# Half of the feed-forward products by Strassen's method, braided with plain ones

## The chip, the core and the metric

The kernel runs on one core of one Trainium2 chip. The metric is device microseconds of one execution. Three runs of the kernel before took 2767.71, 2767.93 and 2768.26 us; the median is 2767.93 us.

## The reference

Two transformer blocks run one after the other on 256 tokens of width 2048, all in float32. Only the feed-forward parts bear on the change:

```
h2 = rmsnorm(x, ffn_norm_g)                                  # first block, D_FF = 5632
x  = x + (silu(h2 @ w_ffn_gate) * (h2 @ w_ffn_up)) @ w_ffn_down

h  = rms_norm(x, g_ff)                                       # second block, D_FF_2 = 8192
x  = x + square(relu(h @ w_ff1)) @ w_ff2
```

`w_ffn_gate`, `w_ffn_up` and `w_ff1` have 2048 rows, so these are the products with K=2048. Ahead of them stand attention, pooling and gates, which the change leaves as they are.

## The kernel before, in words

Every float32 product is made of three fp32r products (`mm3`, L197 to L199): an operand is split into a high part, which fp32r holds exactly, and a low part, which is the rest. x_high w_high + x_high w_low + x_low w_high are added up in PSUM.

The weights come in **pieces** of 256 rows and 512 columns (512 KB). A piece is loaded to a `raw` buffer by a DMA on SP's queue; ScalarE casts it to the high part `wh` (L167); VectorE subtracts to get the low part `wl` (L172); TensorE then does 12 matmuls of 512 columns with it (two K tiles, two token tiles, three products each), with the activations as the stationary operand. A **chunk** is 512 columns of a weight: eight pieces for K=2048, and then an eviction of its two PSUM banks.

All orders are written out by hand (`tc.manual_schedule`). The list `jobs` holds pieces and closures; `drive` walks it, and before the matmuls of piece k it issues the splits up to piece k+4 (`LA`). So on ScalarE's and VectorE's queues the splits of the next four pieces always stand ahead of the eviction that follows piece k. There are five buffers for each of `wh` and `wl`, four PSUM banks for chunks (`acc`) and four for transposes and attention (`aux`).

In the first block's feed-forward, chunks of gate and up alternate, in groups of 4, 4 and 3 pairs; after a pair, its 256 x 512 result is transposed by TensorE (L243, eight transposes to two `aux` banks) and split again, and after a group comes the part of `w_ffn_down` that belongs to it (four chunks of 16 or 12 K tiles). In the second block, four groups of four chunks of `w_ff1` are each followed by four chunks of `w_ff2`. Up's eviction is a VectorE instruction (L750); in the second block ScalarE does the Relu (L1047) and VectorE the square (L1048).

Of the kernel before, what the change touches and what calls it, by code (L numbers as in the profile page):

```python
# [15 lines left out]
P = 128  # L16
S = 256
# [7 lines left out]
LA = 4  # L25
# [43 lines left out]
def body(tc, d, out):  # L69
# [4 lines left out]
    with tc.manual_schedule(), \  # L74
         tc.tile_pool(name="res", bufs=1) as res, \
         tc.tile_pool(name="raw", bufs=RAW) as rawp, \
         tc.tile_pool(name="wh", bufs=LA + 1) as whp, \
         tc.tile_pool(name="wl", bufs=LA + 1) as wlp, \
         tc.tile_pool(name="acc", bufs=4, space=bass.MemoryType.PSUM) as accp, \
         tc.tile_pool(name="aux", bufs=4, space=bass.MemoryType.PSUM) as auxp:  # L80
# [10 lines left out]
        posi = res.tile([P, NT], I32, name="posi")  # L91

# [29 lines left out]
        nacc, naux = [0], [0]  # L122

        def acc_tile():
            nacc[0] += 1
            return accp.tile([P, 512], F32, tag="acc", name=f"acc{nacc[0]}")

        def aux_tile():
            naux[0] += 1
            return auxp.tile([P, 512], F32, tag="aux", name=f"aux{naux[0]}")  # L130

# [6 lines left out]

        def drive():
            pcs = [j for j in jobs if j[0] == "pc"]  # L140
            raws, hl = {}, {}
            nd, ns = [0], [0]

            def dma(upto):
                while nd[0] <= min(upto, len(pcs) - 1):
# [5 lines left out]
                    t = rawp.tile([P, 1024], F32, tag="raw", name=f"raw{i}")  # L151
                    v = t[:, : a * n].rearrange("p (a b) -> p a b", a=a)
                    sync.dma_start(v, src)
                    raws[i] = v
                    nd[0] += 1

            def split(upto):
                while ns[0] <= min(upto, len(pcs) - 1):
                    i = ns[0]
                    dma(i + RAW - 1)  # L160
                    if i in before_split:
                        before_split[i]()
                    v = raws.pop(i)
                    a, n = v.shape[1], v.shape[2]
                    h = whp.tile([P, 1024], F32R, tag="wh", name=f"wh{i}")
                    hv = h[:, : a * n].rearrange("p (a b) -> p a b", a=a)
                    act.copy(hv, v)  # L167
                    lv = None
                    if pcs[i][3]:
                        l = wlp.tile([P, 1024], F32R, tag="wl", name=f"wl{i}")  # L170
                        lv = l[:, : a * n].rearrange("p (a b) -> p a b", a=a)
                        dve.tensor_tensor(lv, v, hv.bitcast(F32), op=ALU.subtract)  # L172
                    hl[i] = (hv, lv)
                    if pcs[i][4]:
                        pcs[i][4](hv, lv)
                    ns[0] += 1

            k = 0
            for j in jobs:
                if j[0] == "run":  # L180
                    j[1]()
                else:
                    split(k + LA)
                    j[2](*hl.pop(k))
                    k += 1

        def piece(src, fn, lo=True, post=None):
            return ("pc", src, fn, lo, post)
# [12 lines left out]
        def chunk(pair, w, kts, c0, n, evict, row0=0, inject=None):  # L201
            """items of pair.T @ w[:, c0:c0+n]; evict(tok, psum) after the last product"""
            items, banks = [], []

            def mk(j):
                def fn(h, l):
                    if j == 0:
                        banks.extend([acc_tile() for _ in range(NT)])
                    for q in range(2):
                        kt = 2 * j + q  # L210
                        for tok in range(NT):
                            mm3(banks[tok][:, :n], pair(kt, tok), (h[:, q, :], l[:, q, :]), kt == 0, kt == kts - 1)
                return fn

            for j in range(kts // 2):
                if inject and j in inject:
                    items.append(("run", inject[j]))
                items.append(piece(wsrc(w, row0 + 2 * j, c0, n), mk(j)))

            def fin():  # L220
                for tok in range(NT):
                    evict(tok, banks[tok][:, :n])
# [3 lines left out]

        def split2(dst_h, dst_l, src, scale=None):
            """dst_h + dst_l = src * scale exactly (scale: a column, or None)"""
# [7 lines left out]
        def transposed(nat, pair, kts, gain=None):  # L236
            """pair[kts] = transposes of nat(tok, i) for the i-th of kts, times gain(kt)"""
# [14 lines left out]
        def rsqrt_mean(o, ss, n):  # L252
            """o = (ss / n + EPS) ** -0.5"""
# [4 lines left out]
        def rsqrt_sum(o, ss, n):  # L258
            """o = (ss + n * EPS) ** -0.5"""
# [7 lines left out]
        # ================= start =================  # L267
# [254 lines left out]
        oT = pairat(A, 0, 16)  # L522
        PS = [X[:, 0:512], X[:, 512:1024]]
# [64 lines left out]
        def s_pair(p):  # L588
# [11 lines left out]
            for h in range(2):  # L600
                for qt in range(NT):
                    j = 2 * qt + h
                    o = slice(qt * S, qt * S + P * (qt + 1))
                    dve.tensor_tensor_reduce(PS[h][:, o], banks[h][:, o], mask[:, (1 - qt) * P :], 1.0, -3e38,
                                             ALU.add, ALU.max, mx[:, j : j + 1])
            dve.scalar_tensor_tensor(nmx, mx, -1.0, rq, ALU.mult, ALU.mult)
            for h in range(2):
                for qt in range(NT):
                    j = 2 * qt + h
                    o = slice(qt * S, qt * S + P * (qt + 1))  # L610
                    act.activation(PS[h][:, o], PS[h][:, o], AF.Exp, bias=nmx[:, j : j + 1], scale=rq[:, j : j + 1],
                                   accum_out=sm[:, j : j + 1])
            dve.reciprocal(rs, sm)
            for h in range(2):
                for qt in range(NT):
                    j = 2 * qt + h
                    o = slice(qt * S, qt * S + P * (qt + 1))
                    dve.tensor_scalar(PS[h][:, o], PS[h][:, o], rs[:, j : j + 1], None, ALU.mult)

        def pt_pair(p):  # L620
            for h in range(2):
                bank = aux_tile()
                for c, o in ((1, 3 * P), (2, 0), (3, 2 * P)):
                    pe.transpose(bank[:, c * P : (c + 1) * P], PS[h][:, o : o + P], ident)  # L624
# [11 lines left out]

        tmp = res.tile([P, 512], F32, name="tmp")
# [55 lines left out]
        def wide(pair, w, ev, tr, pending, kts=16, inject=None, row0=0):  # L693
            """four chunks of 512 columns; the transposes of a chunk run inside the next one"""
# [35 lines left out]
        def t_x(pair, gname):  # L730
            def mk(c):
                return lambda: transposed(lambda tok, i: xnat[:, tok, c * 512 + i * P : c * 512 + (i + 1) * P],
# [4 lines left out]
        pending = wide(mixT, "w_out", ev_res(G[:, 7680:8192], inv2), t_x(h2T, "ffn"), pending)  # L737

# [1 line left out]
        abuf = [rview(G, 1024 * i, NT, 512) for i in range(2)]  # L740

        def ev_silu(c):
            def f(tok, ps):
                act.activation(abuf[c % 2][:, tok, :], ps, AF.Silu, scale=inv2[:, tok : tok + 1])
            return f

        def ev_up(c):
            def f(tok, ps):
                a = abuf[c % 2][:, tok, :]
                dve.scalar_tensor_tensor(a, ps, inv2[:, tok : tok + 1], a, ALU.mult, ALU.mult)  # L750
            return f

        def t_a(aT, c, j):
            return lambda: transposed(blocks(abuf[c % 2]), aT, list(range(4 * j, 4 * j + 4)))
# [10 lines left out]
        for gi, (c0, nch) in enumerate(groups):  # L765
            aT = pairat((C, B)[gi % 2], 0, 16)
            for j in range(nch):
                c = c0 + j
                inj = {}
                if pending is not None:  # L770
                    inj[3 if gi == 0 and j == 0 else 2] = pending
# [375 lines left out]
```

## Time and profile before

| | |
|---|---|
| span of the profiled execution (its own time is not listed apart from it) | 2766.2 us |
| median of the three timed runs | 2767.93 us |
| TensorE busy, of the span | 2759.2 us (100%) |
| weight loads / VectorE / ScalarE busy | 81% / 54% / 47% |
| mean granted TensorE clock | 0.999 |
| DMA | 506.47 MB, 183 GB/s |

TensorE's matmuls overlap one another (each lasts 0.39 us and the next starts 0.23 us after it), so its busy share says only that it hardly ever stands still. Idle time of another engine costs nothing here as long as TensorE waits for none.

### The profile page before, as it was taken

The page shows a single profiled execution, that of the slowest core. Times are in us where ns is not written, and L with a number is a line of the kernel's source. Part 1 is how long each engine was busy: PE and PEld are TensorE (multiplying, and loading weights), DVE is VectorE, ACT ScalarE, POOL GpSimd, SP SyncE. Part 2 cuts the span into 40 slices and gives each one's busy share as a digit, 9 for nine tenths or more (in the row PEclk, how much of TensorE's full clock was granted, in tenths as well). Part 3 has the DMA queues.
Part 4 walks back from the last instruction along what each step waited for, and adds up shares of the span by engine and source line. Part 5 has one row for each costly group of instructions (what it writes and reads, how often), then busy time and mean ns, then how long its engine had stood idle before and what let it go on. Part 6 is the DMA issues. An engine that isn't in the chain of part 4 may idle for free.

```text
span 2766.2 us, 32868 instructions
## 1 busy us (share of the span) xinstructions
PE 2759.2 (100%) x12628; PEld 2249.2 (81%) x12628; DVE 1502.3 (54%) x1717; ACT 1289.0 (47%) x1682; POOL 71.8 (3%) x153
## 2 busy tenths in 40 slices
PE   9999999999999999999999999999999999999999
PEld 8988888888888888888888888888888888888887
DVE  6554677755445454445555475455555455455553
ACT  6544666544443344334455555544444344343442
POOL 1000111000000000000000010000000000000000
PEclk9999999999999999999999999999999999999999
DMA  7665444555555555555555555555555555555554
GB/s 257 214 208 196 158 138 143 176 181 177 190 184 189 185 181 189 184 189 183 183 184 168 191 183 170 181 184 187 181 179 182 190 183 183 188 179 188 183 184 151
DMA packets 143165, 506.47 MB, mean 183 GB/s; under 512 B 16160, under 2 KB 18592, under 8 KB 142496
## 3 DMA queue, kind: packets, MB, share of 16 engines
q1 hardware_dynamic: 142864, 504.31, 53.5%
q8 instruction: 99, 1.62, 0.2%
q14 instruction: 58, 0.48, 0.1%
q10 hardware_dynamic: 144, 0.05, 0.0%
HBM read 502.21 MB, written 2.10 MB: 182 GB/s over the span
## 4 chain that ended last, share of the span: by engine, by line
PE 100%; DMA 0%; DVE 0%; ACT 0%; SPq 0%; issue 0%
PE acc L197 32%; PE acc L198 32%; PE acc L199 31%; PE aux L243 2%; PE aux L197 1%; PE aux L198 1%; PE aux L199 1%; PE aux L578 0%; PE aux L624 0%; DMA raw<-in_w_in_dram 0%; PE aux L461 0%; PE aux L585 0%; PE aux L871 0%; PE aux L867 0%; PE aux L482 0%; PE aux L483 0%
## 5 line engine op out<-in xcount | busy, mean ns | idle before, releaser
L172 DVE TENSOR_TENSOR wl<-raw,wh 128x1024 fp32r<-128x1024 f32 (+2 forms) x947 | 1141.3, 1212 | 1023.4 <-ACT wh L167 1017.6
L167 ACT CAST wh<-raw 128x1024 fp32r<-128x1024 f32 (+1 forms) x950 | 978.4, 1037 | 1091.6 <-PE acc L199 1062.5
L197 PE MATMUL acc<-wh,A 128*128 128x512 f32 (+2 forms) x2336 | 920.6, 394 | 0.7 <-ACT wh L167 0.7
L198 PE MATMUL acc<-wl,A 128*128 128x512 f32 (+2 forms) x2336 | 917.1, 393 | 0.8 <-DVE wl L172 0.8
L199 PE MATMUL acc<-wh,A 128*128 128x512 f32 (+2 forms) x2336 | 917.0, 393 | 0.0
L199 PEld LDWEIGHTS acc<-wh,A 128*128 128x128 f32 x2336 | 438.2, 188 | 102.7
L197 PEld LDWEIGHTS acc<-wh,A 128*128 128x128 f32 x2336 | 438.5, 188 | 100.5 <-ACT wh L167 0.8
L198 PEld LDWEIGHTS acc<-wl,A 128*128 128x128 f32 x2336 | 438.6, 188 | 100.4 <-DVE wl L172 1.1
L197 PE MATMUL acc<-wh,B 128*128 128x512 f32 (+1 forms) x768 | 301.5, 393 | 0.0
L199 PE MATMUL acc<-wh,B 128*128 128x512 f32 (+1 forms) x768 | 299.7, 390 | 0.0
L198 PE MATMUL acc<-wl,B 128*128 128x512 f32 (+1 forms) x768 | 299.7, 390 | 0.0
L197 PE MATMUL acc<-wh,C 128*128 128x512 f32 x672 | 266.6, 397 | 0.0
L199 PE MATMUL acc<-wh,C 128*128 128x512 f32 x672 | 265.5, 395 | 0.0
L198 PE MATMUL acc<-wl,C 128*128 128x512 f32 x672 | 265.4, 395 | 0.0
L197 PEld LDWEIGHTS acc<-wh,B 128*128 128x128 f32 x768 | 144.0, 187 | 32.6
L199 PEld LDWEIGHTS acc<-wh,B 128*128 128x128 f32 x768 | 143.9, 187 | 32.3
L198 PEld LDWEIGHTS acc<-wl,B 128*128 128x128 f32 x768 | 144.1, 188 | 31.6
L199 PEld LDWEIGHTS acc<-wh,C 128*128 128x128 f32 x672 | 125.9, 187 | 30.9
L197 PEld LDWEIGHTS acc<-wh,C 128*128 128x128 f32 x672 | 126.0, 187 | 30.2
L198 PEld LDWEIGHTS acc<-wl,C 128*128 128x128 f32 x672 | 126.0, 188 | 30.1
L230 ACT CAST B<-aux 128x512 fp32r<-128x512 f32 (+1 forms) x56 | 30.1, 575 | 47.3 <-PE aux L243 43.9
L231 DVE TENSOR_TENSOR B<-aux,B 128x512 fp32r<-128x512 f32 (+1 forms) x56 | 35.6, 666 | 29.2 <-ACT B L230 29.2
(191 smaller groups left out, 1149.7 us busy)
## 6 DMA issues: line engine op xcount, KB each, us to landing
raw<-in_w_ff_dram SPq DMA_DIRECT2D x256, 512.0 KB, 3.2
raw<-in_w_in_dram SPq DMA_DIRECT2D x224, 512.0 KB, 4.1
raw<-in_w_ffn_gate_dram SPq DMA_DIRECT2D x88, 512.0 KB, 3.2
raw<-in_w_ffn_up_dram SPq DMA_DIRECT2D x88, 512.0 KB, 3.2
raw<-in_w_ffn_down_dram SPq DMA_DIRECT2D x88, 512.0 KB, 3.2
raw<-in_w_out_dram SPq DMA_DIRECT2D x64, 512.0 KB, 3.3
raw<-in_w_attn_o_dram SPq DMA_DIRECT2D x32, 512.0 KB, 4.0
raw<-in_w_kv_b_dram SPq DMA_DIRECT2D x16, 512.0 KB, 3.4
```

Of the source, the lines that this page charges most:

```text
L167: act.copy(hv, v)
L172: dve.tensor_tensor(lv, v, hv.bitcast(F32), op=ALU.subtract)
L197: pe.matmul(o, x[0], w[0], start=first, stop=False)
L198: pe.matmul(o, x[0], w[1], start=False, stop=False)
L199: pe.matmul(o, x[1], w[0], start=False, stop=last)
L230: act.copy(dst_h, src)
L231: dve.tensor_tensor(dst_l, src, dst_h.bitcast(F32), op=ALU.subtract)
L243: pe.transpose(bank[:, (2 * j + tok) * P : (2 * j + tok + 1) * P], nat(tok, b + j), ident)
```

## The change

**The method.** For `w_ffn_up` and for every second chunk of `w_ff1`, a piece is treated as a 2 x 2 matter: two K tiles by two token tiles of the activations, two K tiles by two halves of 256 columns of the weights. Eight block products become seven (Strassen's method in the form with the fewest additions). Each is three matmuls of 256 columns: a Strassen piece has 21 matmuls of 256 columns, a plain one 12 of 512.

**What the method needs.** VectorE makes four sums of the weight's blocks in place in the loaded piece (three instructions, L203 to L205), so the split is 1792 columns wide for 1024. The activations' four sums are made once (`transposed_s`, into `forms`). The seven products gather in PSUM banks 0 to 3, and after the eighth piece one ScalarE copy and four VectorE additions (L323 to L327) put them together; then comes the eviction.

**The order.** A plain chunk (pieces M0 to M7) and a Strassen chunk (S0 to S7) are braided: M0 M1 S0 M2 S1 M3 S2 M4 S3 M5 S4 M6 S5 M7, eviction of the plain chunk, S6 S7, eviction of the Strassen chunk. There are 11 such braids in the first block and 8 in the second (two to a group). The transposes of the braid before run ahead of S1; in the second block they are those of both chunks, four banks full.

**The buffers.** `wh` and `wl` become one array `W` with slots at fixed places: three slots for M pieces, two for S pieces, and six for pieces outside of braids, which lie on the same ground. The splits run up to three pieces ahead in a braid and four outside, but only as far as the slot's last user is done. In a braid banks 0 to 3 are the Strassen chunk's, 4 and 5 the plain one's, and 6 and 7 are left for transposes. The first chunk after a braid uses banks 2 and 3. Relu and square of the second block are now both ScalarE instructions (L1182, L1183).

```diff
+AHEAD = {PLAIN: 4, MIX: 3, STR: 3}
...
+        FREE = {PLAIN: [0, 1, 2, 3], MIX: [4, 5]}
+        AUX = {PLAIN: (4, 5, 6, 7), MIX: (6, 7)}
...
+        def hslots(kind, n):
+
+            if kind == STR:
+                return (n % 2) * 1792, (2 + n % 2) * 1792, 1792
+            s = n % (3 if kind == MIX else 6)
+            o = 7168 + 1024 * s if s < 3 else 1024 * (s - 3)
+            return o, o + 3072, 1024
...
+            def sums(upto):
+
+                while nt[0] <= min(upto, nd[0] - 1):
+                    i = nt[0]
+                    if pcs[i][5] == STR:
+                        v = raws[i].rearrange("p (a b) -> p a b", a=8)
+                        dve.tensor_tensor(v[:, 4:6, :], v[:, 0:4:3, :], v[:, 1::-1, :], op=ALU.subtract)
+                        dve.tensor_tensor(v[:, 6, :], v[:, 3, :], v[:, 4, :], op=ALU.subtract)
+                        dve.tensor_tensor(v[:, 7, :], v[:, 2, :], v[:, 6, :], op=ALU.subtract)
+                    nt[0] += 1
+
             def split(upto):
-                while ns[0] <= min(upto, len(pcs) - 1):
+                while ns[0] <= min(upto, len(pcs) - 1) and free_h[ns[0]] <= used[0]:
...
+                    sums(i + 2)
...
+        def strassen(pair, forms, w, kts, c0, evict):
...
+            prod = [(("x", 0, 0), 0, 2, 1), (("x", 1, 0), 1, 0, 0), (("s", 3), 2, 3, 0), (("x", 1, 1), 6, 2, 0),
+                    (("s", 0), 3, 1, 1), (("s", 1), 5, 0, 1), (("s", 2), 4, 1, 0)]
...
+                        pe.matmul(o, xh, h[:, wi, :], start=first, stop=False, skip_group_check=True)
+                        pe.matmul(o, xl, h[:, wi, :], start=False, stop=False, skip_group_check=True)
+                        pe.matmul(o, xh, l[:, wi, :], start=False, stop=last, skip_group_check=True)
...
+                act.copy(v[:, 0, :], q[:, 5, :])
+                dve.tensor_tensor(u[:, 0:2, :], v[:, 0:1, :].to_broadcast(bc), q[:, 0:2, :], op=ALU.add)
+                dve.tensor_tensor(u[:, 2:4, :], u[:, 1:2, :].to_broadcast(bc), q[:, 2:4, :], op=ALU.add)
+                dve.tensor_tensor(v[:, ::-1, :], u[:, 2:3, :].to_broadcast(bc), q[:, 3:5, :], op=ALU.add)
+                dve.tensor_tensor(u[:, 3, :], u[:, 3, :], q[:, 6, :], op=ALU.add)
+                evict(0, u[:, 0:4:3, :])
+                evict(1, v)
...
+        def braid(a, b, inject=None):
+
+            pa, pb = [x for x in a if x[0] == "pc"], [x for x in b if x[0] == "pc"]
+            order = [pa[0], pa[1]]
+            for i in range(6):
+                order += [pb[i], pa[i + 2]]
+            order += [a[-1], pb[6], pb[7], b[-1]]
+            for at in sorted(inject or {}, reverse=True):
+                order.insert(at, ("run", inject[at]))
+            return order
...
+                jobs.extend(braid(chunk(h2T, "w_ffn_gate", KT, c * 512, 512, ev_silu, kind=MIX),
+                                  strassen(h2T, h2F, "w_ffn_up", KT, c * 512, ev_up),
+                                  {4: pending} if pending is not None else None))
...
+        def relu2(o, tok, v):
+            act.activation(o, v, AF.Relu, scale=inv4[:, tok : tok + 1])
+            act.activation(o, o, AF.Square)
...
+                jobs.extend(braid(chunk(h2T, "w_ff1_2", KT, c * 512, 512,
+                                        lambda tok, ps: relu2(abuf[:, tok, :], tok, ps), kind=MIX),
+                                  strassen(h2T, h2F, "w_ff1_2", KT, (c + 1) * 512, lambda tok, v: relu2(v, tok, v)),
+                                  {4: pending} if pending is not None else None))
+                pending = two(t_a(aT, blocks(abuf), j), t_a(aT, half, j + 1))
```

**VectorE, second block, where one chunk of `w_ff1` gives way to the next.** In the kernel before, the square (L1048) is followed by two low parts, then by the low parts of the two transposed banks (L231).

```order
L172 TENSOR_TENSOR wl_15490<-raw_15432,wh_15488 128x1024
L1048 TENSOR_TENSOR G<-G 128x512 x2
L172 TENSOR_TENSOR wl_15512<-raw_15450,wh_15510 128x1024
L172 TENSOR_TENSOR wl_15532<-raw_15468,wh_15530 128x1024
L231 TENSOR_TENSOR C<-aux_15546,C 128x512
L231 TENSOR_TENSOR C<-aux_15553,C 128x512
```

In the changed kernel, from the last addition that puts the Strassen chunk together (L327), the rows are the low part of M2, the sums for S2, the low part of S1, that of M3, the sums for S3, the low part of S2, and the four transposed banks (L370).

```order
L327 TENSOR_TENSOR G<-G,PS 128x256
L228 TENSOR_TENSOR W<-R,W 128x1024
L203 TENSOR_TENSOR G<-G 128x512
L204 TENSOR_TENSOR G<-G 128x256
L205 TENSOR_TENSOR G<-G 128x256
L228 TENSOR_TENSOR W<-G,W 128x1792
L228 TENSOR_TENSOR W<-R,W 128x1024
L203 TENSOR_TENSOR G<-G 128x512
L204 TENSOR_TENSOR G<-G 128x256
L205 TENSOR_TENSOR G<-G 128x256
L228 TENSOR_TENSOR W<-G,W 128x1792
L370 TENSOR_TENSOR B<-PS,B 128x512 x4
```

The banks' low parts now stand behind three splits and two sets of sums, and there are four of them on two banks.

**ScalarE at the same place.** Before, the Relu of a chunk stands between casts that were issued ahead.

```order
L167 CAST wh_15652<-raw_15596 128x1024
L1047 ACTIVATE G<-acc_15514,st 128x512
L1047 ACTIVATE G<-acc_15515,st 128x512
L167 CAST wh_15674<-raw_15614 128x1024
L167 CAST wh_15694<-raw_15632 128x1024
L230 CAST C<-aux_15710 128x512
L230 CAST C<-aux_15717 128x512
```

In the changed kernel, the cast of S0 of the next braid is followed by the copy of one product (L323), Relu and square of both token tiles (L1182, L1183), and only then by the cast of M2.

```order
L226 CAST W<-G 128x1792
L323 COPY tmp<-PS 128x256
L1182 ACTIVATE G<-G,st 128x2x256
L1183 ACTIVATE G<-G 128x2x256
L1182 ACTIVATE tmp<-tmp,st 128x512
L1183 ACTIVATE tmp<-tmp 128x512
L226 CAST W<-R 128x1024
L226 CAST W<-G 128x1792
```

Four ScalarE instructions that read what VectorE's additions give now stand ahead of M2's cast.

**VectorE at the end of the first group of the first block**, where `w_ffn_down` begins. Before, the low parts of four of its pieces stand ahead of the eviction of the last chunk (L750).

```order
L172 TENSOR_TENSOR wl_6853<-raw_6795,wh_6851 128x1024
L172 TENSOR_TENSOR wl_6871<-raw_6813,wh_6869 128x1024
L172 TENSOR_TENSOR wl_6889<-raw_6831,wh_6887 128x1024
L172 TENSOR_TENSOR wl_6907<-raw_6849,wh_6905 128x1024
L750 SCALAR_TENSOR_TENSOR G<-acc_6781,st,G 128x512
L750 SCALAR_TENSOR_TENSOR G<-acc_6782,st,G 128x512
```

In the changed kernel, the low parts of S6 and S7 are followed by the additions and by the eviction (L888), and all pieces of `w_ffn_down` stand behind them.

```order
L228 TENSOR_TENSOR W<-G,W 128x1792 x2
L324 TENSOR_TENSOR G<-tmp,PS 128x512
L325 TENSOR_TENSOR G<-G,PS 128x512
L326 TENSOR_TENSOR tmp<-G,PS 128x2x256
L327 TENSOR_TENSOR G<-G,PS 128x256
L888 SCALAR_TENSOR_TENSOR G<-G,st 128x512
L888 SCALAR_TENSOR_TENSOR G<-tmp,st,G 128x512
L228 TENSOR_TENSOR W<-R,W 128x1024 x8
```

No piece of the next weight is split ahead here, since its slot lies on ground that S7 still uses.

## Rows read from the trace of the kernel before

**Rows 1.** The page: engines' busy time and share, and the chain's engines.

```profile
PE 2759.2 (100%) x12628; PEld 2249.2 (81%) x12628; DVE 1502.3 (54%) x1717; ACT 1289.0 (47%) x1682; POOL 71.8 (3%) x153
PE 100%; DMA 0%; DVE 0%; ACT 0%; SPq 0%; issue 0%
```

**Rows 2.** Busy time by stretch: one pair of gate and up with its transposes.

```profile
core 0: us, PE busy (x) PEld busy (x) DVE busy (x) ACT busy (x) POOL busy (x), PEclk, DMA share, GB/s
714.25:759.92 45.67, 45.67 (x202) 36.82 (x201) 22.21 (x20) 19.01 (x20) 0.00 (x0) 1.00 0.52 184
```

**Rows 3.** Timeline of a feed-forward stretch: start, duration, instruction, idle before it.

```profile
1199.63 0.39 PE L199 MATMUL acc<-wh,B 128*128 128x512 f32 x1
...
1200.06 1.05 ACT L167 CAST wh<-raw 128x1024 fp32r<-128x1024 f32 x1 [1.75 <-PE acc L199]
...
1201.14 1.23 DVE L172 TENSOR_TENSOR wl<-raw,wh 128x1024 fp32r<-128x1024 f32 x1 [1.57 <-ACT wh L167]
...
1202.86 1.05 ACT L167 CAST wh<-raw 128x1024 fp32r<-128x1024 f32 x1 [1.75 <-PE acc L199]
```

**Rows 4.** The chain: start, length, link.

```profile
125.97 1.87 PE aux L461 x16
...
536.47 0.87 PE aux L243 x8
```

**Rows 5.** Timeline of the weight loads at L461.

```profile
125.58 2.06 PEld L461 LDWEIGHTS aux<-wh,C 128*128 128x128 f32 x16
```

**Rows 6.** VectorE's groups by shape: count, total us, mean ns, idle before.

```profile
L172 DVE TENSOR_TENSOR wl<-raw,wh 128x1024 fp32r<-128x1024 f32 x907 | 1105.0, 1225 | 1001.6 <-ACT wh L167 995.9
...
L172 DVE TENSOR_TENSOR wl<-raw,wh 128x768 fp32r<-128x768 f32 x24 | 22.7, 965 | 12.4 <-ACT wh L167 12.4
...
L1048 DVE TENSOR_TENSOR G<-G 128x512 f32<-128x512 f32 x32 | 22.1, 692 | 8.4 <-ACT G L1047 8.3
...
L750 DVE SCALAR_TENSOR_TENSOR G<-acc,st,G 128x512 f32<-128x512 f32 x22 | 15.4, 743 | 0.0
L723 DVE TENSOR_TENSOR X<-X,acc 128x512 f32<-128x512 f32 x24 | 15.3, 680 | 0.0
...
L417 DVE TENSOR_TENSOR X<-X 128x256 f32<-128x256 f32 x8 | 3.4, 425 | 0.3
```

**Rows 7.** ScalarE's groups by shape.

```profile
L167 ACT CAST wh<-raw 128x1024 fp32r<-128x1024 f32 x909 | 946.7, 1048 | 1072.5 <-PE acc L199 1050.3 <-issue 8.8 <-DMA raw<-in_w_in_dram 8.1
...
L167 ACT CAST wh<-raw 128x768 fp32r<-128x768 f32 x24 | 19.4, 831 | 7.4 <-PE acc L199 7.4
...
L441 ACT ACTIVATE G<-G 128x512 f32<-128x512 f32 x16 | 10.1, 632 | 14.6 <-DVE G L440 14.3
...
L230 ACT CAST C<-aux 128x256 fp32r<-128x256 f32 x8 | 3.0, 373 | 19.8 <-PE aux L199 19.8
```

**Rows 8.** VectorE's timeline where it has work queued: each row's second number spans all of its xcount.

```profile
44.96 0.20 DVE L338 TENSOR_SCALAR G<-G 128x64 f32<-128x64 f32 x1
45.19 0.20 DVE L339 TENSOR_SCALAR G<-G 128x64 f32<-128x64 f32 x1
...
61.29 3.57 DVE L172 TENSOR_TENSOR wl<-raw,wh 128x768 fp32r<-128x768 f32 x4 [0.24 <-ACT wh L167]
```

**Rows 9.** DMA issues: KB of one, median us from issue to landing.

```profile
raw<-in_w_ff_dram SPq DMA_DIRECT2D x256, 512.0 KB, 3.2
```

**Rows 10.** Timeline of the kernel's start: a wait of TensorE.

```profile
7.76 0.69 PE L198 MATMUL acc<-wl,A 128*128 128x512 f32 x1 [0.76 <-DVE wl L172]
```

**Rows 11.** Busy time by stretch at the start, columns as in Rows 2 (PEclk: granted clock).

```profile
7.00:8.00 1.00, 0.24 (x2) 0.24 (x2) 1.00 (x2) 0.26 (x1) 0.00 (x0) 0.95 1.09 413
8.00:9.00 1.00, 1.00 (x3) 0.81 (x3) 0.50 (x2) 0.06 (x1) 0.00 (x0) 0.50 1.00 376
9.00:10.00 1.00, 1.00 (x4) 0.71 (x4) 0.00 (x0) 1.00 (x2) 0.00 (x0) 0.50 1.10 402
10.00:12.00 2.00, 2.00 (x8) 1.57 (x7) 1.98 (x3) 1.84 (x4) 0.00 (x0) 0.67 1.05 387
12.00:14.00 2.00, 2.00 (x10) 1.63 (x9) 2.00 (x4) 1.82 (x4) 0.00 (x0) 1.00 1.05 385
```

More of the change, by code (lines that the diff above doesn't have):

```diff
@@ L75, in body @@
          tc.tile_pool(name="res", bufs=1) as res, \
[L76 to L80, printed above, removed]
+         tc.tile_pool(name="psum", bufs=1, space=bass.MemoryType.PSUM) as psp:
         A = res.tile([P, 8192], F32R, name="A")
@@ L207, in fn @@
                     if j == 0:
-                        banks.extend([acc_tile() for _ in range(NT)])
+                        banks.extend([FREE[kind].pop(0) for _ in range(NT)])
                     for q in range(2):
@@ L217, in chunk, with mk, fn, fin @@
                     items.append(("run", inject[j]))
-                items.append(piece(wsrc(w, row0 + 2 * j, c0, n), mk(j)))
+                items.append(piece(wsrc(w, row0 + 2 * j, c0, n), mk(j), kind=kind))
             def fin():
                 for tok in range(NT):
-                    evict(tok, banks[tok][:, :n])
+                    evict(tok, bank_at(banks[tok])[:, :n])
+                FREE[kind].extend(banks)
             items.append(("run", fin))
             return items
+        def strassen(pair, forms, w, kts, c0, evict):
+            items = []
+            prod = [(("x", 0, 0), 0, 2, 1), (("x", 1, 0), 1, 0, 0), (("s", 3), 2, 3, 0), (("x", 1, 1), 6, 2, 0),
+                    (("s", 0), 3, 1, 1), (("s", 1), 5, 0, 1), (("s", 2), 4, 1, 0)]
+            def mk(j):
+                def fn(h, l):
+                    opened = set()
+                    for x, wi, bank, half in prod:
+                        o = PS[:, bank * 512 + half * QW : bank * 512 + (half + 1) * QW]
+                        if x[0] == "x":
+                            xh, xl = pair(2 * j + x[1], x[2])
+                        else:
+                            xh, xl = forms[:, 0, j, x[1], :], forms[:, 1, j, x[1], :]
+                        first = j == 0 and bank not in opened
+                        opened.add(bank)
+                        last = j == kts // 2 - 1
+                        pe.matmul(o, xh, h[:, wi, :], start=first, stop=False, skip_group_check=True)
+                        pe.matmul(o, xl, h[:, wi, :], start=False, stop=False, skip_group_check=True)
+                        pe.matmul(o, xh, l[:, wi, :], start=False, stop=last, skip_group_check=True)
+                return fn
+            for j in range(kts // 2):
+                items.append(piece(wsrc(w, 2 * j, c0, 512), mk(j), kind=STR))
+            def fin():
+                q = PS[:, 0:2048].rearrange("p (a b) -> p a b", a=8)
+                u = rview(G, 1024, 4, QW)
+                v = tmp.rearrange("p (a b) -> p a b", a=2)
+                bc = [P, 2, QW]
+                act.copy(v[:, 0, :], q[:, 5, :])
[5 more added lines that the diff above has]
+                evict(1, v)
+            items.append(("run", fin))
+            return items
@@ L736, in body, with ev_silu, ev_up, t_a @@
         h2T = pairat(A, 0, KT)
[L737 to L754, printed above, removed]
+        h2F = rview(C, 0, 2, KT // 2, 4, P)
+        pending = wide(mixT, "w_out", ev_res(tmp, inv2), t_x(h2T, "ffn", h2F), pending)
+        abuf = rview(G, 0, NT, 512)
+        def ev_silu(tok, ps):
+            act.activation(abuf[:, tok, :], ps, AF.Silu, scale=inv2[:, tok : tok + 1])
+        def ev_up(tok, v):
+            a = abuf[:, tok, :].rearrange("p (a b) -> p a b", a=2)
+            dve.scalar_tensor_tensor(a, v, inv2[:, tok : tok + 1], a, ALU.mult, ALU.mult)
+        def t_a(aT, nat, j):
+            return lambda: transposed(nat, aT, list(range(4 * j, 4 * j + 4)))
         def ev_acc(c):
```

173 lines of the change are left out of this document (116 added, 57 removed).

## The prediction

> **What bounds the kernel now.** I read the page first: TensorE is busy for the whole span and the chain of waits is all TensorE [rows 1]. Then the stretches: a pair of gate and up takes 45.67 us, in which VectorE works 22.2 and ScalarE 19.0 [rows 2]. The timeline says how the three fit together: one plain piece every 2.80 us (from cast to cast, 1200.06 to 1202.86), a cast that waits for TensorE to give a slot back and starts 0.04 us after the releasing matmul ends (1199.63 + 0.39), then the low part 1.08 us behind it [rows 3]. So TensorE sets the pace, and the splits run four pieces ahead with half their time to spare. The change takes work from TensorE and gives it to the two others; the question is whether they still come in time.
>
> **What it saves.** A plain piece is 12 matmuls in 2.80 us, 0.233 us each. For 256 columns the chain has 16 matmuls in 1.87 us, 0.117 us each, with a new weight load for each [rows 4]. So a Strassen piece takes 21 x 0.117 = 2.46 us, 0.34 less. There are 19 braids of eight such pieces: 152 x 0.343 = **52.1 us saved**. Eight transposes take 0.87 us as before [rows 4].
>
> One reading speaks against this. A load lasts 0.19 us, and the 16 loads of those 256-column matmuls take 2.06 us together, not 3.0: they overlap one another [rows 5]. The Trainium skill (Perfetto Trace Analysis, Identifying the Most-Contended Engine) says that matmul busy time is a bad measure of headroom and that the busy share of LDWEIGHTS should be used. Taken that way, a Strassen piece would cost its loads; I price that as a rival below. The row is nearer to this change than the rule, so I go by the row.
>
> **Prices on the other engines.** VectorE: 1024 columns 1.225 us, 768 columns 0.965, so 1792 come to 1.225 + 3 x 0.26 = 2.0; the three sums are 0.692 + 2 x 0.425 = 1.54; an addition from PSUM 0.68; up's eviction 0.743 [rows 6]. ScalarE: 1024 columns 1.048 and 768 columns 0.831, so 1792 come to 1.70; an activation from SBUF 0.632; 256 columns from PSUM 0.373 [rows 7]. Four low parts of 768 columns in a row take 3.57 us, not 3.86, so an instruction that needs nothing of the one before starts 0.10 us early; one that needs it starts 0.03 us late (44.96 + 0.20 to 45.19) [rows 8]. The trace has no 1792-column instruction; the two shapes bound the slope, so I add nothing to the range for it. In a queue a plain low part is then 1.13 us, a Strassen one 1.91, its sums 1.50: a pair needs 4.53 of VectorE against 5.26 of TensorE. With additions, up's eviction and transposes, VectorE has about 41 us of work in a braid of 42.9. That is enough in total; what decides is the order in the queues. A weight's DMA lands 3.2 us after issue [rows 9], and a raw slot is given back more than 4.5 us (two low parts and a set of sums) before it is needed, so I cost the DMAs, and the activations' sums ahead of the plain chunks, at nothing.
>
> **Where TensorE waits.** Let T be when TensorE is through with S7. The slot of S7 is that of S5, done 7.72 us before T (M7, S6, S7 follow). From there VectorE needs 0.2 for the release, 1.70 for the cast, 1.91 for S7, 1.50 for sums, 2.25 for M0 and M1, 1.50 for sums and 2.0 for S0: 11.1 us, so the additions begin only at T + 3.4, and end at T + 5.8 (2.43 us, three of them dependent).
>
> *First block, braids after the first (8).* The eviction (1.42) and M2's low part (1.13) bring it to T + 8.4; TensorE needs that after M0, M1, S0 and one matmul, at T + 8.3. Wait 0.2: **1.6 us** in all. The later pieces have more room.
>
> *Second block, second braid of a group (4).* Relu and square start when the additions end: four times 0.66, then M2's cast 1.05 and low part 1.23: T + 10.8, a wait of 2.5. Then TensorE does M2 and fills the two banks left for transposes (T + 14.2). The third bank must wait until VectorE has read the first, and that read stands behind sums, S1, M3, sums and S2: 1.50 + 1.91 + 1.13 + 1.50 + 1.91 = 7.9 from T + 10.8, and 0.69 for the read: T + 19.4. A wait of 5.2. S1 starts at T + 20.5 rather than T + 12.6. **7.9 each, 31.6 us.**
>
> *Ends of groups (7).* With no piece of the next weight split ahead, it stands behind copy, additions, eviction and its own split: first block 0.6 + 2.4 + 1.4 + 1.2 = 5.6, second block 0.6 + 2.4 + 2.7 (Relu, square) + 1.05 + 1.2 = 8.0. TensorE needs it at 0.2, or at 3.0 where one piece is ahead; where three are, it waits only for banks 2 and 3 to be read (2.7). The order has none ahead in the first group of the first block and the second of the second; three in the second and the third; one in the other three. That is 5.4 + 2.7 + 2.6, and 5.0 + 7.8 + 2.7 + 5.0: **31.2 us.**
>
> *Starts of groups.* In the third group of the first block and the fourth of the second, M0's slot is that of the last plain piece. It then stands behind two accumulations and S0's sums (0.2 + 1.3 + 1.5 + 1.2, less the 0.2 that TensorE has): 3.9 each. In the first group of the second block the squares of the norm come ahead too, 5.4; in the first of the first block about 1.4 for the wider split of the last transposes. **14.5 us.** The other three starts have the room.
>
> *The clock.* At the start TensorE, after tiny warm-up matmuls, stands still twice, the second time for 0.76 us [rows 10]; then the granted clock is at 0.50 (1.2 of 2.4 GHz) until about 11.2 us, which costs 0.05 + 0.5 + 0.5 + 0.66 = 1.7 us [rows 11]. The change makes 11 waits of 3.9 to 7.8 us. Whether each lets the clock fall, no row shows: between nothing and 11 x 1.7 = 18.7 us. The row at the start had a weaker load before it, so I take the middle, **9 us**.
>
> **The sum.** 1.6 + 31.6 + 31.2 + 14.5 + 9 = 87.9 lost, 52.1 saved: +35.8 us. The profiled execution's own time is its span, 2766.2, so 2802.0; the median of the runs lies 1.7 above that span: **2804 us**, 1.3% slower.
>
> **The rivals.**
> *Everything hides (faster).* If the low parts that follow a braid's additions came in time, only the 52.1 would be left: 2716 us, or up to 2735 with part of the ends. For it: VectorE's and ScalarE's totals fit in a braid. Against it: the rows of order, in which these low parts stand behind the additions. It decides from the point where all waits together are under 52 us, which means additions, eviction and split some 3 us shorter than the rows make them.
> *Instructions in a queue do not overlap.* With full durations the additions begin at T + 3.8, the second block's late braids lose 8.8, the first block's 1.1: 10.5 us more, 2814; with every wait also dropping the clock, 2823. For it: many of these instructions depend on one another.
> *The third bank does not wait*, if the transposed banks are read earlier than I think: 4 x 5.2 and some of the clock less, 2779.
> *The loads bound.* 21 x 0.188 = 3.95 us for a Strassen piece, 152 x 1.15 = 175 more than a plain one instead of 52 less; the waits inside braids go, those at the ends stay: about 2980. Against it, rows 5. This is the Trainium skill's reading by LDWEIGHTS busy, named above.
> *Same.* It needs waits that add up to the saving within 5.5 us (0.2%, about what a measurement of this kernel can tell from no change); nothing ties the two together.
>
> **How the numbers follow.** The forecast as worked out (2792 to 2813): 0.55. No overlap, or a clock that falls every time (2813 to 2826): 0.19. No wait for the third bank (2774 to 2792): 0.12. Between those and no change: 0.01. Same: 0.03. Faster: 0.08. Loads bound: 0.02. The range from 2774 to 2826 holds the first three, 0.86; its low end leaves out the third-bank wait, its high end takes full durations and all 11 falls of the clock. Slower: 0.55 + 0.19 + 0.12 + 0.01 + 0.02 = 0.89; same 0.03; faster 0.08.
>
> **What would show it.** Strassen matmuls (L310 to L312) 0.117 us apart. In the second block's second braids, TensorE idle before M2 (released by VectorE's low part, with ScalarE's squares ahead of M2's cast) and before the third transposed bank, some 8 us in each. At the ends of groups, idle times of 2.6 to 7.8 us before the first matmuls of `w_ffn_down` and `w_ff2`, longest in the second group of the second block. First braids of a group near 42.1 us without waits. PEclk below 1.00 after some waits. The prediction is wrong if TensorE's idle time in the two feed-forward parts is far below 70 us, if the matmuls of 256 columns are further apart than 0.117, or if VectorE, not its order, fills the braids.

## The result and the profile after

| | before | after |
|---|---|---|
| time, median of 4 runs (us) | 2767.8 (2767.5 to 2768.3) | 2817.2 (2811.6 to 2817.9) |
| ratio, 95% interval | | 1.0175 (1.0161 to 1.0189) |
| profiled execution: time, span (us) | | 2811.6, 2809.8 |
| mean granted clock of TensorE in it | | 0.988 |

The changed kernel is 49.4 us slower; 35.8 were forecast. The profiled execution was the fastest of the four, and the only one with a mean clock of 0.988; the others show 0.985 or 0.986 and spans of 2815.4 to 2816.2. The numbers below are those of the profiled one, whose span is 43.6 us above the 2766.2 of the kernel before.

The page of the changed kernel, busy time and the chain's engines:

```profile
PE 2743.7 (98%) x13996; PEld 2300.2 (82%) x13996; DVE 1853.1 (66%) x2233; ACT 1402.6 (50%) x1749; POOL 72.9 (3%) x153
PE 5%; DVE 0%; ACT 0%; issue 0%; DVEq 0%
```

Against [rows 1] VectorE has 351 us more work and is still idle for a third of the span. The chain no longer runs through TensorE from end to end, and what the walk back covers is 5% of the span. So nothing is read from shares here. The longest waits of TensorE in the sum are these (line waited at, releaser: us in total, times, longest):

```profile
PE PS L258 <- ACT W L226: 16.9, 10, 6.0
PE PS L382 <- DVE B L370: 15.1, 4, 4.9
PE PS L258 <- DVE tmp L326: 15.1, 6, 4.1
PE PS L259 <- DVE W L228: 12.9, 13, 2.4
```

L226 is the cast of a split, L228 its low part, L326 the last but one of the additions, L370 the read of a transposed bank: the four releasers that the prediction names. A Strassen piece has the pace that was priced. Its first and last matmuls, and the plain piece behind it, in the timeline of TensorE:

```profile
722.91 0.28 PE L310 MATMUL PS<-W,A 128*128 128x256 f32 x1
723.03 0.28 PE L311 MATMUL PS<-W,A 128*128 128x256 f32 x1
723.15 0.28 PE L312 MATMUL PS<-W,A 128*128 128x256 f32 x1
...
725.25 0.28 PE L312 MATMUL PS<-W,C 128*128 128x256 f32 x1
725.37 0.39 PE L258 MATMUL PS<-W,A 128*128 128x512 f32 x1
```

From 722.91 to 725.37 are 2.46 us for 21 matmuls. Each lasts 0.28 by its modelled end and starts 0.117 behind the last: starts, not durations, give the pace.

The longest wait shows how the loss is made. The timeline at the end of the second group of the second block, from the last matmul of S7 (without the weight loads):

```profile
2312.78 0.28 PE L312 MATMUL PS<-W,C 128*128 128x256 f32 x1
2312.81 0.69 DVE L324 TENSOR_TENSOR G<-tmp,PS 128x512 f32<-128x512 f32 x1 [3.74 <-PE PS L312]
2313.61 0.69 DVE L325 TENSOR_TENSOR G<-G,PS 128x512 f32<-128x512 f32 x1
2314.33 0.69 DVE L326 TENSOR_TENSOR tmp<-G,PS 128x512 f32<-128x512 f32 x1
2314.93 0.41 DVE L327 TENSOR_TENSOR G<-G,PS 128x256 f32<-128x256 f32 x1
2315.38 0.72 ACT L1182 ACTIVATE G<-G,st 128x512 f32<-128x512 f32 x1 [2.96 <-DVE G L327]
2316.13 0.63 ACT L1183 ACTIVATE G<-G 128x512 f32<-128x512 f32 x1
2316.66 0.70 ACT L1182 ACTIVATE tmp<-tmp,st 128x512 f32<-128x512 f32 x1
2317.40 0.63 ACT L1183 ACTIVATE tmp<-tmp 128x512 f32<-128x512 f32 x1
2317.94 3.87 ACT L226 CAST W<-R 128x1024 fp32r<-128x1024 f32 x4
2319.00 2.36 DVE L228 TENSOR_TENSOR W<-R,W 128x1024 fp32r<-128x1024 f32 x2 [3.66 <-ACT W L226]
2319.02 0.79 PE L258 MATMUL PS<-W,B 128*128 128x512 f32 x1 [5.96 <-ACT W L226]
```

Read it downwards: additions, then Relu and square of two row tiles, then the first of four casts in a row, then TensorE. VectorE idled 3.74 us before the additions and 3.66 after them, ScalarE 2.96: no engine is full, one thing stands behind another. And the first matmul then lasts 0.79 where others last 0.39.

In the second braid of a second-block group TensorE waits three times. These are its rows in the first group: the last matmul of S0, the first two of M2, the first transpose on the third bank.

```profile
2078.24 0.28 PE L312 MATMUL PS<-W,C 128*128 128x256 f32 x1
2079.70 0.51 PE L258 MATMUL PS<-W,A 128*128 128x512 f32 x1 [1.18 <-ACT W L226]
2080.96 0.69 PE L259 MATMUL PS<-W,A 128*128 128x512 f32 x1 [0.75 <-DVE W L228]
...
2089.61 0.33 PE L382 MATMUL PS<-cst,G 128*128 128x128 f32 x1 [3.40 <-DVE B L370]
```

Busy time by stretch (columns as in [rows 2]), at the end of the first group of the first block and around this M2:

```profile
838.00:841.00 3.00, 0.70 (x2) 0.61 (x3) 3.00 (x4) 0.50 (x1) 0.00 (x0) 0.61 0.00 0
841.00:844.00 3.00, 3.00 (x9) 2.32 (x8) 2.65 (x3) 0.24 (x1) 0.00 (x0) 0.50 0.75 240
...
2078.00:2080.00 2.00, 0.82 (x6) 0.50 (x4) 0.32 (x1) 1.97 (x4) 0.00 (x0) 1.00 0.00 0
2080.00:2082.00 2.00, 1.25 (x4) 0.85 (x4) 1.94 (x3) 2.00 (x2) 0.00 (x0) 0.78 0.00 0
2082.00:2084.00 2.00, 2.00 (x6) 1.53 (x5) 2.00 (x2) 1.68 (x2) 0.00 (x0) 0.50 0.00 0
```

Two neighbouring matmuls of M2 three groups later:

```profile
2664.97 0.63 PE L258 MATMUL PS<-W,A 128*128 128x512 f32 x1
2665.40 0.63 PE L259 MATMUL PS<-W,A 128*128 128x512 f32 x1
```

At 2078 TensorE waits 1.2 us for M2's cast and, one matmul later, 0.8 for its low part, and then works at a clock of 0.50 (1.2 of 2.4 GHz). Three groups later the clock is at 0.50 in the same place, and matmuls of 512 columns start 0.43 us apart, where a plain piece has 0.233. The trace has 15 such stretches behind waits.

### The profile page after: what moved, and what is told of

The parts are those of the page before. It is cut to its first block, busy times and chain, and to the rows that moved or that the text cites. A ratio compares the mean times of both kernels' runs of the same rounds, so it can differ in the third digit from the quotient of the medians.

```text
span 2809.8 us, 35965 instructions
## 1 busy us (share of the span) xinstructions
PE 2743.7 (98%) x13996; PEld 2300.2 (82%) x13996; DVE 1853.1 (66%) x2233; ACT 1402.6 (50%) x1749; POOL 72.9 (3%) x153
## 3 DMA queue, kind: packets, MB, share of 16 engines
q1 hardware_dynamic: 142864, 504.31, 52.1%
## 5 line engine op out<-in xcount | busy, mean ns | idle before, releaser
L228 DVE TENSOR_TENSOR W<-R,W 128x1024 fp32r<-128x1024 f32 (+2 forms) x795 | 938.6, 1206 | 431.6 <-ACT W L226 428.8
L226 ACT CAST W<-R 128x1024 fp32r<-128x1024 f32 (+2 forms) x798 | 807.9, 1036 | 522.2 <-PE PS L260 341.1
L258 PE MATMUL PS<-W,A 128*128 128x512 f32 (+2 forms) x1728 | 682.1, 395 | 10.1 <-ACT W L226 10.1
L259 PE MATMUL PS<-W,A 128*128 128x512 f32 (+2 forms) x1728 | 682.4, 395 | 9.0 <-DVE W L228 9.0
L260 PE MATMUL PS<-W,A 128*128 128x512 f32 (+2 forms) x1728 | 680.0, 393 | 0.0
L258 PE MATMUL PS<-W,B 128*128 128x512 f32 (+1 forms) x1248 | 496.3, 398 | 21.9 <-DVE tmp L326 15.1
L259 PE MATMUL PS<-W,B 128*128 128x512 f32 (+1 forms) x1248 | 493.7, 396 | 3.9 <-DVE W L228 3.9
L260 PE MATMUL PS<-W,B 128*128 128x512 f32 (+1 forms) x1248 | 493.5, 395 | 0.0
L226 ACT CAST W<-G 128x1792 fp32r<-128x1792 f32 x152 | 257.3, 1693 | 340.5 <-PE PS L311 153.0
L259 PEld LDWEIGHTS PS<-W,A 128*128 128x128 f32 x1728 | 326.7, 189 | 81.0 <-DVE W L228 14.2
L258 PEld LDWEIGHTS PS<-W,A 128*128 128x128 f32 x1728 | 326.6, 189 | 80.0 <-ACT W L226 12.3
L260 PEld LDWEIGHTS PS<-W,A 128*128 128x128 f32 x1728 | 326.3, 189 | 74.2
L228 DVE TENSOR_TENSOR W<-G,W 128x1792 fp32r<-128x1792 f32 x152 | 307.0, 2020 | 57.4 <-ACT W L226 57.3
L258 PEld LDWEIGHTS PS<-W,B 128*128 128x128 f32 x1248 | 236.5, 190 | 78.4 <-ACT W L226 12.2
L259 PEld LDWEIGHTS PS<-W,B 128*128 128x128 f32 x1248 | 236.5, 189 | 59.4 <-DVE W L228 5.7
L260 PEld LDWEIGHTS PS<-W,B 128*128 128x128 f32 x1248 | 236.3, 189 | 55.3 <-DVE B L370 0.4
L310 PE MATMUL PS<-W,C 128*128 128x256 f32 x608 | 170.7, 281 | 0.0
L312 PE MATMUL PS<-W,C 128*128 128x256 f32 x608 | 170.6, 281 | 0.0
L311 PE MATMUL PS<-W,C 128*128 128x256 f32 x608 | 170.3, 280 | 0.0
L310 PE MATMUL PS<-W,A 128*128 128x256 f32 x456 | 130.6, 286 | 0.0
L312 PE MATMUL PS<-W,A 128*128 128x256 f32 x456 | 128.4, 281 | 0.4 <-DVE W L228 0.4
L311 PE MATMUL PS<-W,A 128*128 128x256 f32 x456 | 128.4, 282 | 0.0
```

The costliest lines, as they stand in the source:

```text
L258: pe.matmul(o, x[0], w[0], start=first, stop=False)
L259: pe.matmul(o, x[0], w[1], start=False, stop=False)
L260: pe.matmul(o, x[1], w[0], start=False, stop=last)
L310: pe.matmul(o, xh, h[:, wi, :], start=first, stop=False, skip_group_check=True)
L311: pe.matmul(o, xl, h[:, wi, :], start=False, stop=False, skip_group_check=True)
L312: pe.matmul(o, xh, l[:, wi, :], start=False, stop=last, skip_group_check=True)
```

## The experiments

Theory: the waits are made by what stands ahead in two queues at three kinds of places (second braids, ends of groups, starts of groups), each can be taken away by itself, and each costs its idle time and often a low clock behind it. Rival: VectorE has too much work in a braid, so a wait taken away comes back. A second rival concerns the clock: that it falls for another reason than the waits. Times are medians; the kernel before had 2767.4 and 2767.6 beside these runs.

| run | us | ratio to before, 95% |
|---|---|---|
| late_pending | 2790.1 | 1.0083 (1.0068 to 1.0098) |
| late_evict | 2792.9 | 1.0094 (1.0077 to 1.0111) |
| own_ground | 2764.0 | 0.9990 (0.9981 to 0.9999) |
| all_three | 2719.8 | 0.9829 (0.9814 to 0.9843) |
| plain_braid | 2767.5 | 0.9999 (0.9990 to 1.0009) |
| only_slots | 2784.6 | 1.0063 (1.0048 to 1.0078) |
| only_banks | 2804.5 | 1.0138 (1.0123 to 1.0153) |
| fill | 2795.0 | 1.0102 (1.0087 to 1.0117) |

**late_pending**: the transposes of the Strassen chunk five places later.

```diff
-                                  {4: pending} if pending is not None else None))
-                pending = two(t_a(aT, blocks(abuf), j), t_a(aT, half, j + 1))
+                                  {4: pending[0], 9: pending[1]} if pending is not None else None))
+                pending = (t_a(aT, blocks(abuf), j), t_a(aT, half, j + 1))
...
+            pending = two(*pending)
             stage(PLAIN)
```

> In the second block's second braids the eight transposes of the Strassen chunk's outputs come five pieces after the eight of the plain chunk, so that the third transposed bank no longer follows the first two at once. Order theory (each wait is made by what stands ahead in VectorE's or ScalarE's queue at that one place, and a wait costs its idle time and a fall of the clock behind it): the four idle times of 3.7 to 5.2 us before the third bank go, 16.2 us, and with them three of the falls of the clock, some 6 us: about 2795 us. Volume theory (VectorE has too much to do in a braid, so a wait taken away at one place comes back at the next): the idle time turns up again in the same braids, and the time stays within 5 us of 2817.

Measured 2790.1, 27 us less; the spans of the two executions with a trace, 2809.8 and 2788.3, are 21.5 apart. Of TensorE's waits, the line for transposed banks is gone; the others stand as they were:

```profile
PE PS L258 <- ACT W L226: 16.9, 10, 6.0
PE PS L258 <- DVE tmp L326: 14.7, 6, 3.8
PE PS L259 <- DVE W L228: 12.9, 12, 2.4
```

Waits of 15.1 us were worth 21.5 by these two traces, whose mean clocks are 0.988 and 0.990: most of the rest is the clock. Nothing came back elsewhere.

**late_evict**: the Strassen chunk's evictions one piece later.

```diff
-                evict(0, u[:, 0:4:3, :])
-                evict(1, v)
+                late.append(lambda: (evict(0, u[:, 0:4:3, :]), evict(1, v)))
...
+        def behind(items):
+            k = [i for i, x in enumerate(items) if x[0] == "pc"][0]
+            return items[: k + 1] + [("run", lambda: late and late.pop()())] + items[k + 1 :]
```

`behind` is put around each braid and each group's first plain chunk.

> The evictions of each Strassen chunk (up's product in the first block, Relu and square in the second) come after the first piece of what follows, so behind the split of that piece's successors, and no longer right behind the additions. Order theory: the waits for M2 go (4 x 2.7), the ends of the second block's groups get 2.7 us shorter each, the first end of the first block 1.4; the third bank may wait 1 us longer, since S1's cast now stands behind Relu and square; with falls of the clock about 25 us in all: 2792 us. Volume theory: within 5 us of 2817.

Measured 2792.9. The waits (L390 and L378 are the old L382 and L370):

```profile
PE PS L390 <- DVE B L378: 21.6, 4, 5.4
PE PS L258 <- DVE tmp L326: 14.7, 6, 4.1
PE PS L259 <- DVE W L228: 8.2, 7, 1.8
PE PS L258 <- ACT W L226: 7.8, 5, 2.5
```

The two lines of the split lose 13.8 us together, and the third bank waits 6.5 longer. That is not because the bank comes later, as was expected of S1's cast. In the timeline of this run the last matmul of S0 and the first on the third bank are 9.35 us apart, where they were 11.37 in the rows above:

```profile
2074.80 0.28 PE L312 MATMUL PS<-W,C 128*128 128x256 f32 x1
...
2084.15 0.47 PE L390 MATMUL PS<-cst,G 128*128 128x128 f32 x1 [5.40 <-DVE B L378]
```

The bank comes 2.0 us sooner (as much in the other three groups), but TensorE, no longer held at M2, is there sooner still. The two waits stand one behind the other, and nearly half of what the first one loses turns up in the second.

**own_ground**: slots by last use, and the gate chunk's banks for the first plain chunk.

```diff
+                if kind != STR and kind != lastk[0]:
+                    cnt[kind] = 0
+                    m = sorted(range(3), key=lambda x: seen_h.get((7168 + 1024 * x) // 256, x - 9))
+                    perm[:] = m if kind == MIX else m + [3, 4, 5]
+                    lastk[0] = kind
...
-            s = n % (3 if kind == MIX else 6)
+            s = perm[n % (3 if kind == MIX else 6)]
...
+                if m == PLAIN:
+                    FREE[PLAIN][:] = [4, 5, 0, 1]
+                    AUX[PLAIN] = (6, 7, 2, 3)
```

> At each change between braids and plain pieces the slots are taken in the order in which their last users end, and the first plain chunk after a braid takes the banks of the gate chunk (free early) instead of Strassen's. Order theory: three plain pieces are split ahead of every braid's additions, so the ends of the first block's groups lose their waits (10.4 us measured) and those of the second block keep some 2.4 us each of 20.1; the starts of groups lose about 10 of 13.4 us; with the clock about 38 us less in all: 2779 us. Volume theory: within 5 us of 2817.

Measured 2764.0, 53 us less, 15 more than expected. The waits (lines 13 further down than after the change):

```profile
PE PS L395 <- DVE B L383: 16.7, 4, 5.0
PE PS L271 <- ACT W L239: 5.3, 5, 1.2
PE PS L272 <- DVE W L241: 4.2, 6, 0.8
```

The waits for additions are gone, and those for splits fell from 29.8 to 9.5, nearly all of it M2's, which this run leaves alone. Two lines are new: 2.6 and 2.4 us, four waits each, for the split of transposed outputs, at the pieces of `w_ff2` that use them. All waits together are some 28 us less, the span 48.1. Most of the rest is the clock, whose mean is 0.995 against 0.988, and which I had put too low.

**only_slots** and **only_banks** take own_ground apart (its diff's first and second half).

> Of the change of slots and banks, the slots alone: pieces are split ahead at every change between braids and plain pieces, but the first plain chunk after a braid still takes Strassen's banks. Order theory: the starts of groups lose their waits (about 12 us) and the ends keep some 2.8 us each, the time until the additions have read the banks (19 of 30 us): 23 us of idle time less and some 10 of the clock, 2784 us. Rival (the banks make the waits at the ends, the slots matter only at the starts): 2795 or more.

> The banks alone: the first plain chunk after a braid takes the gate chunk's banks, but the slots stay as they were, so that in five of seven groups no more than one piece is split ahead. Order theory: only the ends with three pieces ahead (second group of the first block, third of the second) lose their waits, 2.8 and about 4 us, and some of the clock: 2807 us. Rival (the banks make the waits at the ends): some 20 us of idle time less, 2790 or below.

Measured 2784.6 and 2804.5, both within 3 us. With the slots alone all seven ends wait, for the additions to read the banks:

```profile
PE PS L266 <- DVE tmp L334: 18.6, 7, 3.3
```

With the banks alone that line is gone, and the splits wait longer (23.2 and 17.0 against 16.9 and 12.9):

```profile
PE PS L263 <- ACT W L231: 23.2, 12, 6.0
PE PS L264 <- DVE W L233: 17.0, 14, 4.1
```

The ends need both: together they give 53 us, alone 33 and 13.

**all_three**: the three edits above together.

> Late transposes, late evictions and slots by last use together. Order theory: nearly all of the 67 us of idle time and the 23 us that the low clock costs go, and the 53 us that the 256-column products save are left: 2720 to 2735 us, faster than the kernel before (2768). Volume theory: VectorE needs about 41 us of a braid's 42.9, so waits come back somewhere in the braids: above 2760 us.

Measured 2719.8: 97 us less than the change, and 47.6 less than the kernel before. Its page and all waits of TensorE above 0.2 us:

```profile
PE 2709.9 (100%) x13996; PEld 2279.9 (84%) x13996; DVE 1848.0 (68%) x2233; ACT 1400.3 (52%) x1749; POOL 73.9 (3%) x153
```

```profile
PE PS L271 <- ACT W L239: 1.0, 1, 1.0
PE PS L438 <- POOL nh L433: 1.0, 1, 1.0
PE PS L325 <- DVE W L241: 0.8, 2, 0.4
PE PS L272 <- DVE W L241: 0.8, 1, 0.8
```

What is left lies at the kernel's start and at the first S0 of each block. VectorE has the same work as after the change (1848 us), and nobody waits for it. The volume rival is refuted.

**plain_braid**: all_three with the second chunk of a braid by plain products.

```diff
-                                  strassen(h2T, h2F, "w_ffn_up", KT, c * 512, ev_up),
+                                  chunk(h2T, "w_ffn_up", KT, c * 512, 512,
+                                        lambda tok, ps: ev_up(tok, ps.rearrange("p (a b) -> p a b", a=2)), kind=STR),
```

The same for `w_ff1_2`; the sums and the weights' blocks are left out.

> The version with late transposes, late evictions and slots by last use, but the second chunk of each braid done by plain products (12 matmuls of 512 columns a piece, no sums, no additions, plain weights); order, slots, banks and queues of raw weights stay. It measures the saving alone. If a Strassen piece saves 21 x 0.117 against 12 x 0.233 and nothing else: 48 to 53 us above the 2719.8 of the version with all three, so 2768 to 2773, and about the kernel before. If part of the gain of that version lies in the braids or the slots themselves, it is below 2762; if Strassen's pieces saved more than their matmuls, above 2778.

Measured 2767.5, just the kernel before. So the new order, banks and slots cost and bring nothing by themselves, and Strassen's products save 47.7 us once nothing waits.

**fill**: the changed kernel with extra matmuls in the waits.

```diff
+        def busy(n, bank=6, w=None):
+            def f():
+                for _ in range(n):
+                    pe.matmul(bank_at(bank), A[:, 0:P] if w is None else w, A[:, 0:512], start=w is None, stop=w is None,
+                              skip_group_check=True)
+            return f
...
+            run(busy((9, 24, 17, 9)[gi]))
```

> The changed kernel with extra matmuls of 512 columns, whose results nobody reads (or whose weights are zero), put where TensorE waits: 10 before M2 and 14 with zero weights before the third transposed bank in the second block's second braids, 9 to 24 at the ends of groups, 6 to 11 at three starts, each set a little shorter than the wait. Clock theory (a low clock behind the waits costs some 23 us of the profiled run, and it falls because TensorE stood still): the waits stay as long, but most of those 23 us come back: 2793 to 2802 us. Rival (the clock falls for another reason, as the kind of matmul in the braids, or the low stretches are covered by work that would be waited for anyway): no gain, 2815 or more, since the extra matmuls only fill or lengthen waits.

Measured 2795.0, 22.2 us less, with 207 matmuls more. The places above by stretch, the second braid and the longest end:

```profile
2076.00:2080.00 4.00, 4.00 (x19) 3.02 (x18) 3.67 (x5) 3.69 (x4) 0.00 (x0) 1.00 0.00 0
2080.00:2084.00 4.00, 4.00 (x23) 3.37 (x22) 3.93 (x6) 1.86 (x3) 0.00 (x0) 1.00 0.52 146
2086.00:2088.00 2.00, 1.80 (x11) 1.63 (x12) 1.23 (x3) 0.86 (x2) 0.00 (x0) 0.77 0.57 162
2314.00:2318.00 4.00, 3.20 (x13) 2.08 (x12) 0.80 (x1) 3.94 (x6) 0.00 (x0) 1.00 0.00 0
```

TensorE does useless work where it stood still, the clock stays at 1.00 behind most of it, and the kernel is faster. Nothing that it waits for comes earlier: from the last matmul of S0 to the first on the third bank it is 11.4 us in all four groups of this run (2074.84 to 2086.20 in the first), as after the change; and at the longest end the first plain matmul comes 6.24 us behind the last of S7 there and 6.26 here. So the 22.2 us are the clock's alone, and the rival for the clock is refuted. The trace is of the slowest of the four executions (2800.1 us, mean clock 0.996): in it waits of up to 2.4 us are left between the first matmuls of a piece and of up to 1.7 before the third bank, and behind them five of the fifteen stretches at 0.50. The two executions at 0.999, the mean clock of the kernel before, took 2793.4 and 2793.8, so the low clock costs the changed kernel some 22 to 24 us.

## Why the prediction was right, point by point

**The saving** (52.1 forecast): 2.46 us a piece, as priced. Between plain_braid and all_three it is 47.7 us by the medians, 49.0 by the spans (2767.4, of the slowest of plain_braid's ten executions, and 2718.4). A part of the missing 3 to 4 us is at S1: in the timeline of all_three its first matmuls in a second braid start 0.20, 0.24 and 0.23 us apart behind transposes (2057.20, 2057.40, 2057.64, 2057.87) instead of 0.117. What holds them, no run took apart.

**The loads** (the rival at 2980): refuted by the same rows. The Trainium skill (Perfetto Trace Analysis, Identifying the Most-Contended Engine) would judge TensorE's room by MFU (the arithmetic done as a share of the peak) and the busy share of LDWEIGHTS. In all_three that share is 84% while TensorE waits for next to nothing, so here it did not show the bound.

**The waits** (78.9 forecast), from the list of the changed kernel's waits at each place:

| place | forecast | measured |
|---|---|---|
| first block, later braids | 1.6 | 0 |
| second block, second braids (before M2; third bank) | 31.6 (2.5 and 5.2 each) | 23.1 (8.0 and 15.1 in all) |
| ends, first block | 10.7 | 9.1 |
| ends, second block | 20.5 | 16.8 |
| starts | 14.5 | 10.0 |
| sum | 78.9 | 59.0 |

The places were right but for the first row, and so were the releasers; at M2 the cast ends the first wait and the low part the second. The list holds less than what is lost, for two reasons that are in rows. A wait is counted from a modelled end, 0.39 us after the start where the next could start after 0.233, so some 0.16 us of each is not in the list. And the low clock shortens the next wait: the third bank waits 4.9 us in the group where TensorE ran M2 at 1.00, and 3.4 in the three where it ran M2 at 0.50 and came later.

What a second braid loses is therefore better read from T, the end of S7. M0's first matmul starts at 2070.15 in the first group. M2's second matmul, which needs its low part, comes 10.8 us later and the third bank 19.5, in all four groups; T + 10.8 and T + 19.4 were forecast. Without waits the third bank would come at T + 11.7 (three plain pieces, a Strassen one, eight transposes). So these braids lose 7.7 us each, 31 in all, and this price was right, not too high. With 0.16 us for each of the other 19 waits, all waits come to 31 + 35.9 + 3, some 70 us by estimate. Too high were the ends and the starts, above all the ends of the second block with one piece split ahead (2.5 and 3.7 for 5.0); one end came out higher (4.1 for 2.7, the third group of the second block).

**The clock** (9 forecast, bounds 0 and 18.7): this is the term that was mis-sized. The balance of the spans: 43.6 lost, plus 49.0 saved, less some 70 of waits, leaves some 23 for the clock. The run of extra matmuls shows 22.2 by the medians without that balance. Both are above the upper bound. The step that failed is "11 waits of 3.9 to 7.8 us", priced at the middle between no fall and a fall behind each: the clock fell at ten of these eleven places, and also behind five shorter ones (2.0 us in two parts at M2 in three groups of four, and ends of 2.5 and 4.1), which makes 15 falls. At the forecast's 1.7 us each they would be 25.5, so the price of a fall was near and their number was not. Some stretches are longer than the one at the kernel's start (838.6 to 845.5 by the trace's clock; the row from 841 to 844 lies wholly in it). The Trainium skill (TensorE: Matmul & The Clock Gate, Terms) takes the penalty as about the throttled time times one minus the granted share. By the mean clock of 0.988 some 67 us were at half speed, and by that rule the estimate is 34 us. The runs show less than this, 22 to 24: part of the low clock falls on time in which TensorE waits (from 838 to 841 it is busy for 0.70 us of 3.00, at a mean of 0.61), and at M2 it only takes the place of a wait for the third bank.

The two errors are of opposite sign, some 9 too much of waits and some 14 too little of the clock. With 3 less saved and 5.6 more in the median than in the profiled execution they make the 13 us between 2804 and 2817; that the total came so near is in part luck.

**The rivals.** *Everything hides* was wrong for this order of the queues and right in its price: 2716 forecast, 2719.8 with the three edits. *No overlap in a queue* (2814 to 2823) has the right time for a wrong reason: of the additions above, those that need the one before start 0.80 and 0.72 us apart with 0.69 each, but the last, which doesn't, starts after 0.60, and two low parts of a split overlap too (2.36 at 2319.00, where one lasts 1.22). The waits came out as forecast or shorter, not longer, in all places but one end. *The third bank does not wait*: it did, four times.

## What to carry to other kernels

A change that takes work from the engine that bounds the kernel pays in full only if nothing that this engine will need soon stands in another queue behind work that starts when it ends; look for such rows at each change of stage, where fewer pieces are ahead. Mend the order before judging the arithmetic: here the same products were 1.75% slower or 1.7% faster. In this kernel the waits of TensorE cost some 70 us, and the clock that fell behind most of them a third of that again, so price both. But waits that stand one behind the other don't add up: where the later one ends is set by the other engines, as at the third bank, and what comes before it, a wait or a low clock, is hidden in it.

## What the runs showed of the hardware that was not expected

- The granted clock fell to 0.50 behind waits as short as 1.2 and 0.8 us with one matmul between (2078 to 2082), and what it cost in the whole kernel was about a third of what the waits did (22 to 24 us for some 70).
- Matmuls whose result nobody reads, and matmuls with zero weights, held the clock at 1.00 in ten of fifteen places: 207 of them (207 x 0.233 = 48 us of useless work) made the kernel 22.2 us faster.
- Matmuls of 256 columns, each with a weight load of its own, ran 0.117 us apart piece after piece; a run of them behind transposes began with distances of 0.20 to 0.24.
